# A four-layer trunk on one core: tile sizes and pools changed so that matmul operands begin at multiples of 128 bytes, with three steps moved in the feed-forward heads

## The chip, the cores and the metric

The kernel runs on one core of a Trainium2 chip. The metric is device time in microseconds for one execution. Before the change the median of three runs is 2381.13 us (2380.29 to 2392.86). A core has five engines that run side by side, each with an instruction stream of its own: TensorE (PE), VectorE (DVE), ScalarE (ACT), GpSimd (POOL) and SyncE (SP, which here only issues DMA transfers). Every time below comes from these runs, from the profile of one execution, or from its trace.

## What is computed

A batch of one with 512 positions of width 1024 goes through four layers. Each layer adds a mixer's output to `x` and then a gated feed-forward network (FFN):

```python
for layer in range(4):
    h = rmsnorm(x, norm_mix[layer])
    x = x + mixer(h)              # layers 0 and 3: S5; 1: GLA; 2: differential attention
    h = rmsnorm(x, norm_ffn[layer])
    g, u = split(h @ w_gate_up, 2)   # 1024 x 5632
    x = x + (silu(g) * u) @ w_down   # 2816 x 1024
return rmsnorm(x, norm_final)
```

All arrays are fp32. The S5 mixer is a diagonal state-space scan followed by a 1024 x 2048 product, GLA a gated linear attention with products of 1024 x 3088 and 1024 x 1024, the attention one with products of 1024 x 3072 and 1024 x 1024.

## The kernel before

**Products.** A large product is done in the type fp32r. Each operand is split into a high part and a remainder, and three matmuls (high by high, high by low, low by high) add up in PSUM: `mm3`, lines 349 to 353. A matmul has two SBUF operands. The stationary one is loaded into the array (128 columns, LDWEIGHTS), the moving one is streamed past it. In the profile a row `acc<-whl,act` names first what is written, then the moving operand (`whl`), then the stationary one (`act`).

- `gemm_b` (and `gemm_units`, its form as a generator): moving is a weight tile `whl` of 512 columns, stationary the activations (`act`, `hT`, `zT` or `oT`).
- `gemm_a`: moving is `hT`, the transposed normalised activations, 512 columns wide, and stationary the weights `whl`.
- `seven_product` (line 566): moving is a `side` of 256 columns, stationary the weights.

Weights come from HBM as fp32 (`staged`, tag `wst`), ACT casts the high part (line 334) and DVE subtracts it for the low part (line 338), both into `whl`.

**FFN of layers 1 to 3.** `ffn` computes the gate and up product with Strassen-like sums: seven half-size products instead of eight for each of 11 blocks of 256 hidden columns. `seven_block` gives the steps of a block: products `one` to `seven`, with sides "11", "1", "2", "12", "3", "4", "22" of the activations. Each product is 24 matmuls, so a block has 168. The sides "11" and "12" lie in a tile `sides` in the pool `hp`; the others, named `side1` and so on, lie in the FFN's own pool. The first two blocks ("heads" a and b) are interleaved in an order written out by hand, the string `plan` in `ffn`, and `hand_all` makes all engines keep that order until `hand()` gives it back to the scheduler. In `plan`, `split`, `high` and `low` are the ACT and DVE halves of making an operand, `add22` and `add21` are sums of weight tiles on DVE, `total1` to `total4` are sums of activation quarters on DVE, and `one:a` is product one of block a. After each 4, 4 and 3 blocks a `gemm_b` of the down projection runs. Some weight tiles are loaded twice, the second time by POOL's queue with an addition in flight (`load` with `plus`): names `room1` and `summed`.

**Turned x.** Layer 3 wants the rows of `x` in another order. `turn_x` (layer 2 only) writes `x` to DRAM and reads it back in the new order, 2 MB each way, and the same with the small `r`; all four DMAs go to POOL's queue, and the two that read wait there for those that write. It is called at block 2, tied behind the last adding DMA of that block by `issue_after`.

**Memory.** Pools are laid out one after another in SBUF in the order of `Trunk.__init__`: const, xp, hp, wp, normp (`np_`), small (`sp`), then the pool of the stage at work. A tile takes a multiple of 32 bytes in each partition. In front of const lie 8192 bytes of DMA scratch. The const pool adds up to 6080 bytes: four constants of the framework 128, `ident` 512, `mhalf` 32, `ones` 512, three columns 96, six S5 tables 1536, `pw` 2048, `dcol` 64, `mrow` 512, `mask16` 64, two rotation tables 512, two columns 64. That is 47 x 128 + 64, so xp begins 64 bytes past a multiple of 128, and so do hp, wp and every tile in them, whose sizes are multiples of 128. The table gives where each operand lies, as bytes past a multiple of 128:

| operand | pool | before | after the change |
|---|---|---|---|
| `whl` (weights), `hT`, `sides`, `x` | wp, hp, xp | 64 | 0 |
| `hh` (what is transposed) | normp | 64 | 0 |
| `act`, `side1` to `side22`, `oT` | stage pools | 0 | 0 |
| `zT` (S5) | right end of SBUF | 96 | 0 |
| `wa2`, `aT`, `kd`, `v`, `st`, `walr` (GLA) | gla | 32 | 0 |
| `X`, `Q`, `cs` of the first S5 layer | s5_0 | 32 | 0 |
| `X`, `Q` of the second, made beside layer 0's FFN | ffn0 | 64 | 0 |

The stage pools begin at a multiple of 128 before and after.

Of the kernel before, what the change touches and what calls it, by code (L numbers as in the profile page):

```python
# [21 lines left out]
P = 128  # L22
# [38 lines left out]
class Left:  # L61
# [84 lines left out]
class Sides(Left):  # L146
# [18 lines left out]
    def ahead(self, n):  # L165
# [3 lines left out]
        if len(self.heads) == 2:  # L169
            self.total("3")  # L170
# [49 lines left out]
class Chunks:  # L220
# [3 lines left out]
    def __init__(self, tr, grow):  # L224
# [3 lines left out]
        self.ms = tr.np_.tile([P, 2, NT], F32, tag="msq", name="msq")  # L228
# [13 lines left out]
    def finish(self):  # L242
# [6 lines left out]
        r = tr.np_.tile([P, NT], F32, tag="rcol", name="rcol")  # L249
# [13 lines left out]
class Trunk:  # L263
    def __init__(self, ctx, tc, ins, out):
# [177 lines left out]
    def normed(self, xt, g, out, pool, aside=False):  # L442
# [6 lines left out]
        ms = self.sp.tile([P, 1], F32, tag="ms", name="ms")  # L449
# [121 lines left out]
    def seven_block(self, fp, slots, left, wgu, b, turn):  # L571
# [20 lines left out]
        def load(name, q, half, plus=None, room=None):  # L592
# [8 lines left out]
            if plus:  # L601
                self.added = nc.gpsimd.dma_start(w[:], left.quarter(*plus, b), accum_op=ALU.add)
# [109 lines left out]
    def ffn(self, l, left, after=None, turn=False, aside=None):  # L712
# [5 lines left out]
        with self.tc.tile_pool(name=f"ffn{l}", bufs=1, reuse_waits="tile") as fp:  # L718
# [14 lines left out]
            for w, n, *room in (  # L733
# [6 lines left out]
                split21a one:a split21b square flush one:b total1 one_out:a finish high1 low1 total2 split1a high2 low2  # L740
                one_out:b two:a two:b split1b high3 two_out:a five:a add22a highSa two_out:b lowSa five_out:a five:b
                add22b highSb diag lowSb low3 split3a six:a spread five_out:b rows six:b six_out:a split3b seven:a
                six_out:b total4 split22a high4 low4 seven:b seven_out:a split22b three:a seven_out:b gate1:a gate1:b
                high22 low22 three:b add21a highFa add21b lowFa highFb lowFb four:a four:b three_out:a three_out:b
            """
            for step in plan.split():
# [11 lines left out]
                elif name == "flush":  # L758
                    self.flush()
                else:  # L760
# [7 lines left out]
            for nb in (4, 4, 3):  # L768
                acts = []
                for n in range(b0, b0 + nb):  # L770
# [29 lines left out]
    def turn_x(self, r):  # L800
# [8 lines left out]
        r = self.np_.tile([P, NT], F32, tag="rcol", name="rturned")  # L809
# [147 lines left out]
    def s5_rows_of_phases(self, p, cp, fhi, flo, f):  # L957
# [31 lines left out]
        self.mmagic = cp.tile([P, 1], F32, name="mmagic")  # L989
# [212 lines left out]
    def s5_spilled(self, pool, L):  # L1202
# [5 lines left out]
        rs = pool.tile([P, 1, 112], F32, name="rssp")  # L1208
# [172 lines left out]
    def s5_first(self, ctx):  # L1381
# [3 lines left out]
        zT = zpool.tile([P, 2, KT, SEQ], F32R, name="zT")  # L1385
# [752 lines left out]
```

## Time and profile before

The profiled execution took 2382.31 us, of which the span in the trace, from the first to the last instruction, is 2380.6 us.

| engine | busy us | share of the span |
|---|---|---|
| DVE | 1487.1 | 62% |
| ACT | 1073.0 | 45% |
| POOL | 266.8 | 11% |

The TensorE clock granted is 0.98 of full speed over the span. The core reads 275.92 MB from HBM and writes 23.99 MB. The line for TensorE and the rows for the largest groups stand in the prediction. A row of groups gives the line of the source, the engine, the operation, the names, the shape (partitions x elements), the number of instructions, then the busy time in us and the mean ns of one, and behind the second bar the idle time before them and what ended it. Matmuls overlap in the pipeline, so the mean duration of one (some 390 ns) isn't what it costs; that is the distance from one start to the next. A row of the timeline gives the start in us, the length in us, the engine, line, operation, names, shape and the count of merged instructions, and in brackets the idle time before it with its releaser.

### The profile page before, as it was taken

The page shows a single profiled execution, that of the slowest core. Times are in us where ns is not written, and L with a number is a line of the kernel's source. Part 1 is how long each engine was busy: PE and PEld are TensorE (multiplying, and loading weights), DVE is VectorE, ACT ScalarE, POOL GpSimd, SP SyncE. Part 2 cuts the span into 40 slices and gives each one's busy share as a digit, 9 for nine tenths or more (in the row PEclk, how much of TensorE's full clock was granted, in tenths as well). Part 3 has the DMA queues.
Part 4 walks back from the last instruction along what each step waited for, and adds up shares of the span by engine and source line. Part 5 has one row for each costly group of instructions (what it writes and reads, how often), then busy time and mean ns, then how long its engine had stood idle before and what let it go on. Part 6 is the DMA issues. An engine that isn't in the chain of part 4 may idle for free. (4 is left out here: it accounts for less than half of the span.)

```text
span 2380.6 us, 35208 instructions
## 1 busy us (share of the span) xinstructions
PE 2269.0 (95%) x14055; PEld 1962.8 (82%) x14055; DVE 1487.1 (62%) x2311; ACT 1073.0 (45%) x1749; POOL 266.8 (11%) x335
## 2 busy tenths in 40 slices
PE   4799999999999999999999998989999899999997
PEld 3578888788877789898987887888989788999996
DVE  7774565555443459585753666875847874967674
ACT  4463445444352346252544665653635233634442
POOL 3330100111000011010001221110000000101000
PEclk9699999999999999999999999999999899999999
DMA  4123344544332258564345465694732645666521
GB/s 110 34 52 138 95 138 143 166 129 166 118 103 85 71 143 208 137 177 124 111 142 117 107 133 145 170 243 115 195 98 89 214 158 150 170 179 154 162 76 67
DMA packets 275502, 317.42 MB, mean 133 GB/s; under 512 B 45653, under 2 KB 214377, under 8 KB 274058
## 3 DMA queue, kind: packets, MB, share of 16 engines
q1 hardware_dynamic: 227210, 238.14, 31.9%
q0 software_dynamic: 48128, 77.02, 15.7%
q8 instruction: 111, 1.82, 0.3%
q14 instruction: 53, 0.43, 0.1%
HBM read 275.92 MB, written 23.99 MB: 126 GB/s over the span
## 5 line engine op out<-in xcount | busy, mean ns | idle before, releaser
L338 DVE TENSOR_TENSOR whl<-wst,whl 128x1024 fp32r<-128x1024 f32 x294 | 359.0, 1223 | 363.1 <-ACT whl L334 362.3
L334 ACT CAST whl<-wst 128x1024 fp32r<-128x1024 f32 x294 | 308.4, 1050 | 530.5 <-PE acc L353 354.8
L566 PE MATMUL a<-side,whl 128*128 128x256 f32 x2376 | 291.2, 279 | 14.2 <-ACT r L638 6.0
L566 PEld LDWEIGHTS a<-side,whl 128*128 128x128 f32 x2376 | 281.4, 190 | 16.2 <-ACT whl L334 6.9
L351 PE MATMUL acc<-whl,act 128*128 128x512 f32 x704 | 276.5, 393 | 0.7 <-DVE g L611 0.7
L353 PE MATMUL acc<-whl,act 128*128 128x512 f32 x704 | 276.9, 393 | 0.0
L352 PE MATMUL acc<-whl,act 128*128 128x512 f32 x704 | 275.6, 391 | 0.0
L566 PE MATMUL c<-side,whl 128*128 128x256 f32 x1584 | 192.4, 278 | 3.6 <-DVE whl L338 3.6
L566 PEld LDWEIGHTS c<-side,whl 128*128 128x128 f32 x1584 | 186.9, 189 | 4.0 <-DVE whl L338 4.0
L351 PEld LDWEIGHTS acc<-whl,act 128*128 128x128 f32 x704 | 132.2, 188 | 30.9 <-DVE g L611 1.9
L352 PEld LDWEIGHTS acc<-whl,act 128*128 128x128 f32 x704 | 132.2, 188 | 28.8
L353 PEld LDWEIGHTS acc<-whl,act 128*128 128x128 f32 x704 | 132.3, 188 | 27.9
L351 PE MATMUL any<-hT,whl 128*128 128x512 f32 x384 | 151.7, 395 | 0.0
L352 PE MATMUL any<-hT,whl 128*128 128x512 f32 x384 | 149.6, 390 | 0.0
L353 PE MATMUL any<-hT,whl 128*128 128x512 f32 x384 | 149.6, 389 | 0.0
L351 PE MATMUL acc<-whl,hT 128*128 128x512 f32 x352 | 143.8, 408 | 1.1 <-ACT whl L334 0.6
L352 PE MATMUL acc<-whl,hT 128*128 128x512 f32 x352 | 138.6, 394 | 1.0 <-DVE whl L338 1.0
L353 PE MATMUL acc<-whl,hT 128*128 128x512 f32 x352 | 139.0, 395 | 0.0
L338 DVE TENSOR_TENSOR whl<-halves,whl 128x1024 fp32r<-128x1024 f32 x72 | 87.7, 1222 | 32.5 <-ACT whl L334 32.5
L352 PE MATMUL acc<-whl,zT 128*128 128x512 f32 x256 | 103.9, 406 | 4.1 <-DVE whl L338 4.1
L334 ACT CAST whl<-halves 128x1024 fp32r<-128x1024 f32 x72 | 75.3, 1052 | 69.2 <-PE acc L353 26.7
L351 PE MATMUL acc<-whl,zT 128*128 128x512 f32 x256 | 102.8, 406 | 2.7 <-ACT zT L468 2.7
(438 smaller groups left out, 4185.1 us busy)
## 6 DMA issues: line engine op xcount, KB each, us to landing
wst<-in_ffn_w_gate_up_dram SPq DMA_DIRECT2D x110, 512.0 KB, 4.0
wst<-in_ffn_w_down_dram SPq DMA_DIRECT2D x88, 512.0 KB, 3.7
halves<-in_ffn_w_gate_up_dram SPq DMA_DIRECT2D x42, 512.0 KB, 5.9
slot<-in_ffn_w_gate_up_dram SPq DMA_DIRECT2D x39, 512.0 KB, 6.6
wst<-in_ffn_w_gate_up_dram POOLq DMA_DIRECT2D x33, 512.0 KB, 6.4
wst<-in_s_w_glu_dram SPq DMA_DIRECT2D x32, 512.0 KB, 3.6
spill<-opsp POOLq DMA_DIRECT2D x8, 2048.0 KB, 8.7
wst<-in_gla_w_in_dram SPq DMA_DIRECT2D x24, 512.0 KB, 3.6
```

The source lines that it names most:

```text
L334: self.nc.scalar.copy(hl[:, 0], w[:])
L338: self.nc.vector.tensor_tensor(hl[:, 1], w[:], hl[:, 0].bitcast(F32), op=ALU.subtract)
L351: mm(out, lh, rh, start=first, stop=False)
L352: mm(out, lh, rl, start=False, stop=False)
L353: mm(out, ll, rh, start=False, stop=last)
L566: mm(o, hl[:, x, k, c], side[:, y, k], start=first and not (j or k or n), stop=k == 3 and n == 2, skip_group_check=True,)
```

## The change

Constants: `ones` is put ahead of `mhalf`, and `mhalf` grows from 8 to 24 columns (32 to 96 bytes), so the const pool is 6144 bytes, 48 x 128. The small tiles `msq` and `rcol` go from normp to the pool small, whose tile `ms` gets 6 buffers instead of 8: small goes from 1856 to 1920 bytes, normp loses 128. `mmagic`, `ind` and `rssp` are made wider (to 128, 128 and 512 bytes) and used as before. Behind `zT` at the right end of SBUF lies a new unused tile `edge` of 96 bytes.

Order in the FFN heads: `high22` and `low22` (side 22) come ahead of `three:a`, with `add21a` and its `high` and `low` behind them; before, they came after both `gate1` steps. `total3` is no longer called inside `ahead`: layers 1 and 3 call it right after `ahead(2)`, and layer 2 calls it in `plan`, ahead of `total1`. At the end of the attention layer the two evacuations `evac(0)` and `evac(1)` come two matmul groups sooner, and each `ahead(1)` follows the evacuation of its row block.

x's copy: `turn_x` is called in `plan`, behind `five:b`, instead of at block 2.

```diff
-        self.ms = tr.np_.tile([P, 2, NT], F32, tag="msq", name="msq")
-        self.r = tr.np_.tile([P, NT], F32, tag="rcol", name="rcol")
+        self.ms = tr.sp.tile([P, 2, NT], F32, tag="msq", name="msq", bufs=2)
+        self.r = tr.sp.tile([P, NT], F32, tag="rcol", name="rcol", bufs=2)
...
         self.heads += [self.tr.halves(y, 4, 256) for y in w]
-        if len(self.heads) == 2:
-            self.total("3")
...
-        self.mhalf = self.cp.tile([P, 8], F32, name="mhalf")
+        self.ones = self.cp.tile([P, P], F32, name="ones")
+        self.mhalf = self.cp.tile([P, 24], F32, name="mhalf")
         nc.vector.memset(self.mhalf[:], -0.5)
-        self.ones = self.cp.tile([P, P], F32, name="ones")
...
-        ms = self.sp.tile([P, 1], F32, tag="ms", name="ms")
+        ms = self.sp.tile([P, 1], F32, tag="ms", name="ms", bufs=6)
...
-                self.added = nc.gpsimd.dma_start(w[:], left.quarter(*plus, b), accum_op=ALU.add)
+                nc.gpsimd.dma_start(w[:], left.quarter(*plus, b), accum_op=ALU.add)
...
-                split21a one:a split21b square flush one:b total1 one_out:a finish high1 low1 total2 split1a high2 low2
+                split21a one:a split21b square flush one:b total3 total1 one_out:a finish high1 low1 total2 split1a high2 low2
                 one_out:b two:a two:b split1b high3 two_out:a five:a add22a highSa two_out:b lowSa five_out:a five:b
-                add22b highSb diag lowSb low3 split3a six:a spread five_out:b rows six:b six_out:a split3b seven:a
-                six_out:b total4 split22a high4 low4 seven:b seven_out:a split22b three:a seven_out:b gate1:a gate1:b
-                high22 low22 three:b add21a highFa add21b lowFa highFb lowFb four:a four:b three_out:a three_out:b
+                turn add22b highSb diag lowSb low3 split3a six:a spread five_out:b rows six:b six_out:a split3b seven:a
+                six_out:b total4 split22a high4 low4 seven:b seven_out:a split22b high22 low22 three:a add21a highFa
+                seven_out:b lowFa add21b gate1:a highFb three:b lowFb gate1:b four:a four:b three_out:a three_out:b
             """
+            if l != 2:
+                plan = plan.replace("total3", "")
...
+                elif name == "turn":
+                    r = self.turn_x(left.r) if turn else r
...
-                    if turn and n == 2:
-
-                        with self.tc.issue_after(self.added.ins):
-                            r = self.turn_x(left.r)
...
-        self.mmagic = cp.tile([P, 1], F32, name="mmagic")
+        self.mmagic = cp.tile([P, 32], F32, name="mmagic")[:, :1]
...
-        rs = pool.tile([P, 1, 112], F32, name="rssp")
+        rs = pool.tile([P, 1, 128], F32, name="rssp")[:, :, :112]
...
         zT = zpool.tile([P, 2, KT, SEQ], F32R, name="zT")
+        zpool.tile([P, 24], F32, name="edge")
...
-                ahead = (lambda: nxt.ahead(2)) if L and d else None
+                ahead = (lambda: (nxt.ahead(2), nxt.total("3"))) if L and d else None
...
-            ind = p.tile([P, 2], F32, name="ind")
+            ind = p.tile([P, 32], F32, name="ind")[:, :2]
...
-                2: {1: (one,), 3: (one, lambda: evac(0, banks[0])), 5: (one, lambda: evac(1, banks[1])), 7: (one,)},
-                3: {1: (one,), 3: (one, lambda: nxt[0].ahead(1)), 5: (one,)},
+                2: {1: (one, lambda: evac(0, banks[0])), 3: (lambda: evac(1, banks[1]), one), 5: (one,), 7: (one,)},
+                3: {1: (one,), 3: (one,), 5: (one,)},
...
                 evac(t, banks[t])
-                if t == 2:
-                    nxt[0].ahead(1)
+                nxt[0].ahead(1)
```

More of the change, by code (lines that the diff above doesn't have):

```diff
@@ L248, in finish @@
         v.tensor_scalar_add(ms[:], ms[:], 1e-6)
-        r = tr.np_.tile([P, NT], F32, tag="rcol", name="rcol")
+        r = tr.sp.tile([P, NT], F32, tag="rcol", name="rcol", bufs=2)
         nc.gpsimd.tensor_tensor(r[:], ms[:], tr.mhalf[:, :NT], op=ALU.pow)
@@ L808, in turn_x @@
         nc.gpsimd.dma_start(d[:].rearrange("(t p) -> p t", p=P), r[:])
-        r = self.np_.tile([P, NT], F32, tag="rcol", name="rturned")
+        r = self.sp.tile([P, NT], F32, tag="rcol", name="rturned", bufs=2)
         nc.gpsimd.dma_start(r[:], d[:].rearrange("(p t) -> p t", t=NT))
@@ L1465, in s5_second @@
         zT = zpool.tile([P, 2, KT, SEQ], F32R, name="zT")
+        zpool.tile([P, 24], F32, name="edge")
         with self.tc.tile_pool(name="s5_1", bufs=1) as p:
```

4 lines of the change are left out of this document (2 added, 2 removed).

## The prediction

> **What bounds the kernel now.** I read the page first: which engine is busy, and which groups make it so.
>
> ```profile
> span 2380.6 us, 35208 instructions
> PE 2269.0 (95%) x14055; PEld 1962.8 (82%) x14055; DVE 1487.1 (62%) x2311; ACT 1073.0 (45%) x1749; POOL 266.8 (11%) x335
> L566 PE MATMUL a<-side,whl 128*128 128x256 f32 x2376 | 291.2, 279 | 14.2 <-ACT r L638 6.0
> L566 PE MATMUL c<-side,whl 128*128 128x256 f32 x1584 | 192.4, 278 | 3.6 <-DVE whl L338 3.6
> L351 PE MATMUL acc<-whl,act 128*128 128x512 f32 x704 | 276.5, 393 | 0.7 <-DVE g L611 0.7
> L351 PE MATMUL any<-hT,whl 128*128 128x512 f32 x384 | 151.7, 395 | 0.0
> L351 PE MATMUL acc<-whl,hT 128*128 128x512 f32 x352 | 143.8, 408 | 1.1 <-ACT whl L334 0.6
> L351 PE MATMUL acc<-whl,zT 128*128 128x512 f32 x256 | 102.8, 406 | 2.7 <-ACT zT L468 2.7
> ```
>
> TensorE is the bound, and its own matmuls follow each other without a wait. Lines 351 to 353 go together, so the 512-wide groups count 2112 (`act`), 1152 (`any`), 1056 (`hT`) and 768 (`zT`). The list with shapes kept apart gives the rest: 1584 matmuls with `sides`, 384 with `oT`.
>
> ```profile
> L566 PE MATMUL a<-sides,whl 128*128 128x256 f32 x792 | 100.3, 283 | 0.0
> L566 PE MATMUL d<-sides,whl 128*128 128x256 f32 x792 | 100.0, 283 | 0.9 <-ACT whl L334 0.9
> L351 PE MATMUL acc<-whl,oT 128*128 128x512 f32 x128 | 53.4, 417 | 2.4 <-ACT oT L468 2.4
> ```
>
> What one costs is the distance between starts, read from the timeline.
>
> ```profile
> 229.04 0.40 PE L351 MATMUL acc<-whl,zT 128*128 128x512 f32 x1
> 235.34 0.40 PE L351 MATMUL acc<-whl,zT 128*128 128x512 f32 x1
> ...
> 284.97 0.39 PE L351 MATMUL any<-hT,whl 128*128 128x512 f32 x1
> 291.09 0.39 PE L351 MATMUL any<-hT,whl 128*128 128x512 f32 x1
> ...
> 882.86 5.92 PE L566 MATMUL d<-sides,whl 128*128 128x256 f32 x48
> 888.62 5.62 PE L566 MATMUL c<-side,whl 128*128 128x256 f32 x48
> 894.08 2.89 PE L566 MATMUL a<-side,whl 128*128 128x256 f32 x24
> ...
> 984.46 0.39 PE L351 MATMUL acc<-whl,act 128*128 128x512 f32 x1
> 991.33 0.39 PE L351 MATMUL acc<-whl,act 128*128 128x512 f32 x1
> ```
>
> Between the pairs lie 27, 27, 48, 48 and 30 matmuls: `zT` 233.3 ns, `any` 226.7, `d<-sides` 120.0, `c<-side` 113.75, `act` 229.0. The middle pair decides: same shape, same weights pool, back to back; `sides` begins 64 bytes past a multiple of 128, `side` at one, and it costs 6.25 ns less. From 120.0 and 226.7, both 64 off, 256 more columns cost 106.7 ns. So 256 columns cost 106.7, 32 columns (128 bytes) 13.3, and the fixed part is 13.3 where the moving operand is off, as if one more stretch of 128 bytes were read, and 7.0 where it is aligned.
>
> **Part 1, the layout.** Afterwards both operands lie at 0. No row shows that pair for fp32r. The fixed part F lies between 0 (columns don't stream faster than in these rows) and 7.0 (moving at 0, weights still at 64). The lowest 512-wide distance is the one with both operands at the same phase (`any`, 64 and 64), while `act` (64 and 0) and `zT` (64 and 96) cost more; equal phases will hold everywhere afterwards, so I go below 7.0, to the middle: F = 3.3. Then a 512-wide matmul costs 216.7 and a 256-wide one 110.0. The gains: `zT` 16.6, `any` 10.0, `hT` taken as `any` 10.0, `act` 12.3, `oT` taken as `act` 12.3, `sides` 10.0, `side` 3.75.
>
> [...]
>
> Not all of it passes on. These rows show where another engine is near:
>
> ```profile
> 879.91:960.98 81.07, 77.03 (x660) 76.00 (x658) 72.05 (x83) 48.16 (x62) 10.06 (x8) 1.00 0.77 197
> 1508.11:1600.44 92.33, 80.79 (x659) 79.83 (x658) 76.42 (x91) 53.24 (x70) 12.78 (x12) 0.94 0.89 234
> 2028.87:2110.30 81.43, 78.25 (x660) 77.43 (x659) 73.06 (x84) 50.11 (x64) 10.06 (x8) 0.98 0.78 198
> ...
> 1400.00:1475.00 75.00, 67.40 (x398) 54.67 (x397) 55.70 (x151) 55.17 (x154) 15.70 (x22) 1.00 0.48 115
> 1858.00:1950.00 92.00, 82.92 (x585) 76.21 (x582) 82.81 (x119) 22.84 (x35) 1.05 (x1) 0.93 0.64 228
> ```
>
> Columns: stretch, length, then busy PE, PEld, DVE, ACT, POOL, granted clock, DMA share, GB/s. The first three are the stretches of blocks 0 to 3 in the three FFNs; DVE is busy 72 to 76 us there, so I count half. In the attention PE has gaps (67.4 of 75): 60%. In the S5 pipe of layer 3 DVE works 82.8 of 92 us; the 192 `zT` matmuls of the two pipes count nothing. Elsewhere all passes.
>
> - `zT`: 576 x 16.6 ns = 9.6 us
> - `any`: 1152 x 10.0 = 11.5
> - `hT`: 480 in GLA, 4.8; 576 in the attention, 5.8 x 0.6 = 3.5
> - `act`: 2112 x 12.3 = 26.0
> - `oT`: 192 in GLA, 2.4; 192 in the attention, 1.4
> - FFN blocks: 1584 x 10.0 + 3960 x 3.75 = 30.7; 4 of 11 blocks count half: 25.1
>
> Sum 84.3 us, on about 9500 matmuls that pass on; each ns of F is worth 9.5 us. F = 0 would add 31, F = 7.0 take 35. The wider tiles and `edge` add no instruction; one memset at the start, of `mhalf`, grows by 16 columns, before TensorE has its first work. The tiles moved between the small pools keep two buffers, and `ms` with six has at most four users in a row (the four row blocks of a norm), so no wait comes of it. What is left of TensorE's work (transposes, scores, the S5 matmuls in plain fp32) I count at nothing: those groups are small, none is among the eight rows above, and a gain there would fall mostly into the attention and the S5 pipes, whose rows follow.
>
> **Part 2, the heads.**
>
> ```profile
> 909.88 1.22 DVE L217 TENSOR_TENSOR side<-halves,side 128x1024 fp32r<-128x1024 f32 x1 [1.64 <-ACT side L212]
> ...
> 913.43 0.50 PE L566 MATMUL a<-side,whl 128*128 128x256 f32 x2 [1.95 <-ACT whl L334]
> 914.69 5.49 PE L566 MATMUL a<-side,whl 128*128 128x256 f32 x46 [0.76 <-DVE whl L338]
> 924.12 2.77 PE L566 MATMUL c<-side,whl 128*128 128x256 f32 x22 [0.84 <-DVE whl L338]
> ```
>
> `four:a` waits 2.7 us for side 22 and the sum of weights, because both are made after `gate1`. Made sooner, they are there when `three` ends. But the next wait, at 924.12, is for DVE's own queue, which had stood idle only 1.64 us; the remaining work on it is the same. I count 1.3 per head (between 0 and 2.7), 3.9 for three. At the end of the attention `total3` and the second head's split stood ahead of the last evacuation, and the transposes behind it waited:
>
> ```profile
> 1507.72 0.63 PE L108 MATMUL tp<-ident,hh 128*128 128x128 f32 x4 [1.69 <-ACT sq L99]
> ```
>
> Without them it falls away: 1.5 (0 to 1.7); `total3` then stands on DVE ahead of `total1`, whose product comes 5 us later.
>
> **Part 3, x's copy.** The FFN of layer 2 has 92.3 us in that stretch, the other two 81.1 and 81.4. What is late:
>
> ```profile
> 1511.41 1.03 POOL L126 TENSOR_TENSOR rcol<-ms,mhalf 128x4 f32<-128x4 f32 x1 [3.74 <-DVE ms L125]
> 1518.73 1.33 POOL L602 DMA_DIRECT2D halves<-in_ffn_w_gate_up_dram  x1 [6.29 <-DMA halves<-in_ffn_w_gate_up_dram]
> ...
> 1533.68 1.30 POOL L804 DMA_DIRECT2D xturn<-vall  x1
> 1555.97 0.57 POOL L806 DMA_DIRECT2D x<-xturn  x1 [12.53 <-DMA xturn<-vall]
> 1571.35 1.29 POOL L602 DMA_DIRECT2D wst<-in_ffn_w_gate_up_dram  x1 [9.24 <-DMA slot<-in_ffn_w_gate_up_dram]
> ...
> 1543.82 1.05 ACT L334 CAST whl<-halves 128x1024 fp32r<-128x1024 f32 x1
> ...
> 1580.64 1.04 ACT L334 CAST whl<-wst 128x1024 fp32r<-128x1024 f32 x1 [7.09 <-DMA wst<-in_ffn_w_gate_up_dram]
> ...
> 1584.54 5.02 PE L566 MATMUL a<-side,whl 128*128 128x256 f32 x24 [6.04 <-ACT r L638]
> ...
> 1520.00:1530.00 10.00, 10.00 (x89) 9.93 (x88) 8.95 (x14) 6.99 (x10) 0.05 (x1) 1.00 0.39 64
> 1540.00:1550.00 10.00, 7.39 (x62) 7.18 (x63) 9.97 (x14) 7.36 (x11) 1.32 (x1) 1.00 1.09 349
> ```
>
> The copy out took 22 us amid full DMA engines (1.09), and the weight tile that PE needed came late; the wait also lowered the clock (24 matmuls took 5.02 us). Moved behind `five:b` the copy goes to POOL right behind `r` (1511.41), so all four DMAs start from about 1512.4, and run while the share is 0.39 (1520 to 1530). On POOL's queue block 2's first adding DMA now stands behind them, until the copy out has landed; In the profile it went out at 1518.73, before the copy, and ACT took its tile at 1543.82. A copy out of 12 us from 1512.4 on lets it go at about 1525, 6 us later; with some 9 us for a load of that kind (the 9.24 us wait in the row at 1571.35) it lands near 1534, 10 us early. If the copy out took 22 us again, it would land about when it is needed. SP's loads pass by POOL's queue and only share the DMA engines; those issued between 1512 and 1535 belong to blocks 2 and 3. Where `x` is next used, the first `gemm_b`, lies 65 us later. I take 10 of the 11.2 us, between -2 (that tile a little late, and nothing won) and 11.2.
>
> **Sum.** Against the profiled execution's own 2382.3 us (the median of the runs, 2381.1, is 1.2 below it): 84.3 + 3.9 + 1.5 + 10 = 99.7, so 2282 us.
>
> **Rivals.**
> - *Phases don't matter to each other*: F stays 7.0, as the aligned row has it. For it: it is the only aligned row. Against: `act` and `zT` differ though both have the same moving tile. 2282 + 35 = 2318 us.
> - *A stationary operand at 0 is itself dearer*, by the 2.3 ns that `act` stands above `any`: F = 9.3, 2282 + 57 = 2339 us.
> - *The change does not do what it says*: what separates `d` and `c` is their pool, not the phase, and only parts 2 and 3 bring anything: 2382 - 15 = 2367 us. Against it: the difference is close to half of 13.3 ns. [...]
> - *Slower*: both operands beginning on the same phase 0 collide, and each matmul pays one stretch (13.3 ns) above the aligned row: F = 20.3, (20.3 - 3.3) x 9.5 = 162 us above my forecast: 2444 us. It decides from F = 13.8, where the 99.7 us of the sum are used up. Against it: with both at phase 64 nothing above the 13.3 is seen.
>
> **Chances and range.** My forecast 0.58, with its own range 2248 (F = 0) to 2318; F at 7.0 0.25; stationary dearer 0.09; no effect of the phase 0.04; slower 0.04. The range 2248 to 2345 takes in the first three. What can be told from no change is about 0.5%, 12 us. All but the last case are faster by more, 2367 only just, so I give faster 0.94, same 0.02, slower 0.04.
>
> **What would show it.** In the trace after: `d<-sides` and `c<-side` at the same distance, 107 to 114 ns; all 512-wide groups within 2 ns of each other between 213 and 220; the three FFN stretches alike at 77 to 80 us; no wait over 1 us at `four:a`; the copy out landing in 12 us. Wrong would be 512-wide distances that stay at 227 and above, a 256-wide one above 114, or PE waiting for block 2's `five`.

## The result and the profile after

The changed kernel took 2399.97 us (median of 9 runs, 2395.45 to 2402.79), the kernel before 2383.86 (9 runs, 2380.29 to 2392.86): ratio 1.0063, 95% interval 1.0049 to 1.0076. It became 0.6% slower, clear of the spread of the runs. The profiled execution took 2402.79 us, its span is 2401.1: 20.5 above before.

The page of the changed kernel, engines first, then the groups (line numbers are 2 lower than before: `seven_product` is L564, `mm3` L349 to L351):

```profile
span 2401.1 us, 35215 instructions
PE 2292.8 (95%) x14055; PEld 1980.7 (82%) x14055; DVE 1488.0 (62%) x2311; ACT 1073.9 (45%) x1749; POOL 267.3 (11%) x335
L564 PE MATMUL a<-side,whl 128*128 128x256 f32 x2376 | 298.8, 282 | 2.5 <-DVE whl L336 2.5
L564 PE MATMUL c<-side,whl 128*128 128x256 f32 x1584 | 202.5, 285 | 10.6 <-DVE whl L336 10.6
```

The count of matmuls is the same and TensorE is busy 23.8 us longer: the time is in the matmuls themselves, and in the groups that were to gain. Idle time moved too: `a<-side` waits 2.5 us in all instead of 14.2, `c<-side` 10.6 instead of 3.6. The distances come from the timeline of the same kernel:

```profile
284.77 0.39 PE L349 MATMUL any<-hT,whl 128*128 128x512 f32 x1
289.08 0.39 PE L350 MATMUL any<-hT,whl 128*128 128x512 f32 x1
...
885.19 5.92 PE L564 MATMUL d<-sides,whl 128*128 128x256 f32 x48
890.95 5.86 PE L564 MATMUL c<-side,whl 128*128 128x256 f32 x48
896.65 3.01 PE L564 MATMUL a<-side,whl 128*128 128x256 f32 x24
...
983.75 0.39 PE L349 MATMUL acc<-whl,act 128*128 128x512 f32 x1
990.03 0.39 PE L349 MATMUL acc<-whl,act 128*128 128x512 f32 x1
```

Between the rows lie 19, 48, 48 (from 890.95 to 896.65) and 27 starts: `any` 226.8 ns (before 226.7), `d` 120.0 (120.0), `c` 118.75 (113.75), `act` 232.6 (229.0). What was to become shorter stayed, and `side` and `act` became longer.

By stage, windows of before, then of the changed kernel: the rows at 1005.75 and 1010.95 are blocks 4 to 7 of FFN1, where TensorE has no gap; those at 882.23, 1520.24 and 2041.17 the stretches of blocks 0 to 3, which the prediction has as 81.07, 92.33 and 81.43.

```profile
1005.75:1083.19 77.44, 77.44 (x673) 77.43 (x672) 61.49 (x69) 43.78 (x54) 7.73 (x6) 1.00 0.71 184
```

```profile
1010.95:1090.89 79.94, 79.94 (x674) 79.94 (x673) 61.66 (x69) 43.48 (x54) 7.73 (x6) 1.00 0.69 178
...
882.23:965.29 83.06, 79.14 (x659) 78.34 (x658) 72.00 (x83) 47.68 (x62) 10.05 (x8) 1.00 0.76 199
1520.24:1607.96 87.72, 81.61 (x659) 80.79 (x658) 77.73 (x93) 52.85 (x70) 12.78 (x12) 0.96 0.94 238
2041.17:2124.65 83.48, 80.01 (x659) 79.59 (x658) 72.29 (x84) 49.71 (x64) 10.03 (x8) 0.98 0.77 199
```

Only the stretch with x's copy is shorter (-4.6); the other two are 2 us longer. In it POOL and TensorE look like this (a line of three dots stands for rows left out):

```profile
1526.00 0.83 POOL L802 DMA_DIRECT2D xturn<-vall  x1
...
1538.12 1.08 POOL L804 DMA_DIRECT2D x<-xturn  x1
...
1555.83 0.56 POOL L808 DMA_DIRECT2D rturned<-rturn  x1 [15.84 <-DMA rturn<-rcol]
...
1563.39 0.40 PE L564 MATMUL c<-side,whl 128*128 128x256 f32 x2
1568.56 5.06 PE L564 MATMUL c<-side,whl 128*128 128x256 f32 x22 [4.77 <-DVE whl L336]
```

The copy out took 12 us (1526.00 to 1538.12) where it had taken 22, and the 6.04 us wait of before is gone. In its place stands a wait of 4.77 us ahead of block 2's `five`, and the 22 matmuls behind it took 5.06 us instead of 2.8.

### The profile page after: what moved, and what is told of

It reads as the page before. It is cut to its first block, busy times and chain, and to the rows that moved or that the text cites. A ratio compares the mean times of both kernels' runs of the same rounds, so it can differ in the third digit from the quotient of the medians.

```text
span 2401.1 us, 35215 instructions
## 1 busy us (share of the span) xinstructions
PE 2292.8 (95%) x14055; PEld 1980.7 (82%) x14055; DVE 1488.0 (62%) x2311; ACT 1073.9 (45%) x1749; POOL 267.3 (11%) x335
## 5 line engine op out<-in xcount | busy, mean ns | idle before, releaser
L564 PE MATMUL a<-side,whl 128*128 128x256 f32 x2376 | 298.8, 282 | 2.5 <-DVE whl L336 2.5
L564 PEld LDWEIGHTS a<-side,whl 128*128 128x128 f32 x2376 | 289.0, 189 | 3.5 <-DVE whl L336 3.3
L349 PE MATMUL acc<-whl,act 128*128 128x512 f32 x704 | 279.6, 397 | 1.1 <-DVE g L609 1.0
L351 PE MATMUL acc<-whl,act 128*128 128x512 f32 x704 | 278.0, 395 | 0.0
L564 PE MATMUL c<-side,whl 128*128 128x256 f32 x1584 | 202.5, 285 | 10.6 <-DVE whl L336 10.6
L564 PEld LDWEIGHTS c<-side,whl 128*128 128x128 f32 x1584 | 195.9, 192 | 11.4 <-DVE whl L336 11.4
L349 PEld LDWEIGHTS acc<-whl,act 128*128 128x128 f32 x704 | 132.6, 188 | 33.3 <-DVE g L609 2.3
L351 PEld LDWEIGHTS acc<-whl,act 128*128 128x128 f32 x704 | 132.6, 188 | 30.9
L349 PE MATMUL any<-hT,whl 128*128 128x512 f32 x384 | 151.7, 395 | 0.0
L351 PE MATMUL any<-hT,whl 128*128 128x512 f32 x384 | 149.6, 390 | 0.0
L349 PE MATMUL acc<-whl,hT 128*128 128x512 f32 x352 | 144.2, 410 | 1.3 <-DVE ro L1863 0.7
L351 PE MATMUL acc<-whl,hT 128*128 128x512 f32 x352 | 139.1, 395 | 0.0
L349 PE MATMUL acc<-whl,zT 128*128 128x512 f32 x256 | 102.6, 405 | 2.8 <-ACT zT L466 2.8
```

What stands on the lines that cost most here:

```text
L349: mm(out, lh, rh, start=first, stop=False)
L351: mm(out, ll, rh, start=False, stop=last)
L564: mm(o, hl[:, x, k, c], side[:, y, k], start=first and not (j or k or n), stop=k == 3 and n == 2, skip_group_check=True,)
```

## Experiments

Below, "distance" between addresses means the byte address of the moving operand less that of the stationary one, modulo 256, and a mean start distance is the mean over all starts of a class that follow each other without a wait.

**Each half by itself.** `e1_order_alone` is the changed kernel with every line of the layout as before; `e2_layout_alone` is the kernel before with those lines as changed.

```diff
  e1: the changed kernel, and
-        self.ones = self.cp.tile([P, P], F32, name="ones")
-        self.mhalf = self.cp.tile([P, 24], F32, name="mhalf")
+        self.mhalf = self.cp.tile([P, 8], F32, name="mhalf")
...
-        zpool.tile([P, 24], F32, name="edge")
  e2: the kernel before, and the same lines the other way
```

> The changed order (heads, attention's end, x's copy) on the layout of before. Theory P (the cost hangs on where the moving operand lies against the stationary one, not on either address alone) and theory S (a stationary operand at a multiple of 128 is dear) both put all of the loss on the layout: 256-wide matmuls with side at 113 to 114 ns as before, act at 229, and the time 5 to 9 us below before, some 2376 us, from the FFN heads. Theory O (the new order loses the time): 2390 us or more, with the layout's rows as before.

> The new layout on the order of before. Theories P and S: side 119 to 121 ns, act 232, zT 232 to 233, hT and any 227 to 228 as before; the time 21 to 26 us above before, some 2406 us. Theory O: within 5 us of before.

| run | median us (before beside it) | ratio, 95% interval |
|---|---|---|
| order alone | 2376.32 (2387.11) | 0.9961 (0.9945 to 0.9978) |
| layout alone | 2407.54 (2387.11) | 1.0086 (1.0060 to 1.0112) |

The layout costs 0.86% and the new order gains 0.39%; the two add up to 0.47%, and the change measured 0.63%, within the intervals. So the whole loss lies in the layout. In the layout run the mean start distances are those of the changed kernel: `side` 118.7 (order alone 113.9), `act` 232.6 (229.0), `oT` 232.6 (229.3), `any` 227.4 (227.3), `hT` 228.1 (228.1), `zT` 232.6 (233.2), `sides` 119.6 (119.4). Times their counts that is 3960 x 4.8 + 2112 x 3.6 + 384 x 3.3 + 1584 x 0.2 - 768 x 0.6 = 28 us, beside 26.1 between the spans (2406.7 and 2380.6).

The gain of the order isn't where its expectation put it, in the FFN heads. By windows of its trace the stretches of blocks 0 to 3 take 81.58, 86.38 and 82.05 us (before 81.07, 92.33 and 81.43): 6 us come from the stretch with x's copy, and the other two are 0.5 and 0.6 us longer. The profiled execution was the longest of the ten (2383.15 us), so its span shows none of the gain.

**What makes `side` dearer.** The layout moved the weights by 64 bytes and left `side` where it was. Either a stationary operand at 0 is dear in itself, or only the distance counts. `e3_stage64` keeps the weights at 0 and moves all stage pools up by 64 bytes:

```diff
         self.dp = ep("dram", 1, space=DRAM)
+        self.sp.tile([P, 16], F32, tag="spad", name="spad", bufs=1)
```

> The changed kernel with one unused tile of 64 bytes at the end of the pool small, so that the stage pools (side, act, oT) begin 64 past a multiple of 128 and the weights stay at 0. Theory P: the distance between side and weights modulo 128 is that of before again (64), so side falls back to 113 to 114 ns and act to 229; 2400 - 25 - 6 = about 2369 us. Theory S: the stationary weights still lie at 0, side stays at 119 to 121 ns; act, whose stationary operand is now at 64, falls to 227; about 2395 us.

Its timeline in FFN1, then its window of blocks 4 to 7 there:

```profile
887.47 5.62 PE L565 MATMUL c<-side,whl 128*128 128x256 f32 x48
892.93 2.88 PE L565 MATMUL a<-side,whl 128*128 128x256 f32 x24
```

```profile
1004.30:1081.97 77.67, 77.67 (x673) 77.67 (x672) 61.03 (x68) 43.70 (x54) 7.73 (x6) 1.00 0.72 183
```

`c` is back at 113.75, blocks 4 to 7 at 77.67, `act` at 229.0, and the kernel at 2378.88, 0.9964 (0.9951 to 0.9976). One unused tile of 64 bytes takes back the whole loss. It is the distance that counts.

**Then `sides` too.** If -64 is good for 256 columns, the large buffers with `sides` should lie 64 under the weights. `e4_hp64` is order alone with const 64 bytes shorter (three one-column tiles merged) and 64 bytes of room ahead of the weights, so that xp and hp lie 64 lower. It also keeps `edge`, so that `zT` lies at distance 64:

```diff
-        self.halfpi = cp.tile([P, 1], F32, name="halfpi")
+        cols = cp.tile([P, 3], F32, name="cols")
+        self.halfpi = cols[:, 0:1]
...
         self.wp = ep("wp", 3)
+        self.wp.tile([P, 16], F32, tag="wpad", name="wpad", bufs=1)
```

> The changed order on the layout of before, with the pools xp and hp (hT, sides) 64 bytes lower while the weights stay 64 past a multiple of 128, and zT at 0 instead of 96. Theory P: sides falls from 120 to 113 to 114 ns, any from 226.7 to about 220, hT (moving and stationary swapped) rises to about 229, zT falls from 233 to 229; 1584 x 6.3 + 1152 x 6.7 + 576 x 4.2 - 1056 x 2.3 ns = 17.7 us, so 14 to 18 us below the run with the order alone, some 2360 us. Theory S has the same for sides and any, because their weights stay at 64, and leaves hT at 227 or lets it rise to 229. A theory by which only the pool matters: sides stays at 120 and the time at 2376 us.

The timeline of `any`, then the window of blocks 4 to 7 of FFN1:

```profile
286.74 0.40 PE L350 MATMUL any<-hT,whl 128*128 128x512 f32 x1
293.04 0.39 PE L350 MATMUL any<-hT,whl 128*128 128x512 f32 x1
```

```profile
1015.51:1091.69 76.18, 76.18 (x673) 76.18 (x672) 59.82 (x67) 42.78 (x54) 7.73 (x6) 1.00 0.73 186
```

`sides` fell from 119.4 to 114.1 and blocks 4 to 7 to 76.18. But `any`, which reads the same buffers 512 wide, rose from 227.3 to 233.3 (6.30 us over 27 starts): 1152 x 6 = 7 us given back of the 1584 x 5.3 = 8.4. `hT` as the stationary operand rose from 228.1 to 229.4, 1 us, and `zT` fell from 233.2 to 229.4, 3 us. That leaves some 3 us, which the times can't tell from nothing: 2378.11, 0.9967 (0.9948 to 0.9985), beside 0.9961 of order alone. The 14 to 18 us expected were a miss: what is good for 256 columns is bad for 512.

**A table of distances.** `e5_phases` leaves the whole trunk out. It loads two tiles, and reads them in groups of 48 matmuls, 512 wide and 256 wide in turn, while the moving operand goes up in steps of 32 bytes:

```diff
+    for s in (0, 16, 8):
+        for m in range(0, 128, 8) if s == 0 else range(0, 128, 16):
+            wide(m, s)
+            narrow(m, s)
```

> The disputed cost by itself: the whole trunk is left out, and fp32r matmuls run back to back in the pattern of line 349 to 353 (two stationary tiles, two moving ones), in groups of 48 with 512 moving columns and 48 with 256, with the moving operand moved on by 32 bytes from pair of groups to pair, 0 to 480, against a stationary operand at 0, then by 64 bytes against one at 64 and at 32. Theory P: the same distance gives the same spacing whatever the stationary address; at equal phases 120 ns (256 columns) and 226.7 (512), at a distance of -64 (448) 113 to 114 and about 233, at +64 229 for 512. A theory in which the address of the stationary operand counts by itself: the rows with it at 64 differ from those with it at 0 at equal distance by 3 ns or more. Theory P leaves open where the least of each curve lies: if it is below 113 and 226, a better layout than either kernel's follows.

The timeline: three pairs of groups with the stationary operand at 0, at distances 0, 64 and 192, then the two 256-wide groups at distance -64 with the stationary operand at 64:

```profile
30.13 11.07 PE L43 MATMUL acc<-mov,sta 128*128 128x512 f32 x48
41.04 5.92 PE L53 MATMUL acc<-mov,sta 128*128 128x256 f32 x48
46.79 11.36 PE L43 MATMUL acc<-mov,sta 128*128 128x512 f32 x48
...
63.59 11.15 PE L43 MATMUL acc<-mov,sta 128*128 128x512 f32 x48
74.58 5.60 PE L53 MATMUL acc<-mov,sta 128*128 128x256 f32 x48
80.02 11.37 PE L43 MATMUL acc<-mov,sta 128*128 128x512 f32 x48
...
130.83 11.37 PE L43 MATMUL acc<-mov,sta 128*128 128x512 f32 x48
142.03 5.61 PE L53 MATMUL acc<-mov,sta 128*128 128x256 f32 x48
147.47 11.35 PE L43 MATMUL acc<-mov,sta 128*128 128x512 f32 x48
...
309.76 5.62 PE L53 MATMUL acc<-mov,sta 128*128 128x256 f32 x48
315.22 11.06 PE L43 MATMUL acc<-mov,sta 128*128 128x512 f32 x48
...
376.76 5.82 PE L53 MATMUL acc<-mov,sta 128*128 128x256 f32 x48
382.42 11.06 PE L43 MATMUL acc<-mov,sta 128*128 128x512 f32 x48
```

Each start less the one before, over 48 (10.91 / 48 = 227.3 and 5.75 / 48 = 119.8 for distance 0), gives with the stationary operand at 0:

| distance | 0 | 32 | 64 | 96 | 128 | 160 | 192 (-64) | 224 (-32) |
|---|---|---|---|---|---|---|---|---|
| 512 wide, ns | 227.3 | 233.3 | 229.0 | 233.5 | 233.3 | 234.2 | 233.3 | 233.1 |
| 256 wide, ns | 119.8 | 116.7 | 113.3 | 120.0 | 118.8 | 118.8 | 113.3 | 118.5 |

The second 256 bytes repeat the first (distance 256: 226.9 and 120.0). Every class of before and after fits its column: `any` at 0, `act` at 64 and then 128, `side` at -64 and then 128, `sides` at 0. With the stationary operand at 64, distance 0 is alike (226.9 and 119.8), but +64 costs 233.4 and 117.8, so distance isn't all of it. And -64 has two readings there: 113.75 ns the first time, with the moving operand at 0 (309.76 to 315.22), and 117.9 the second time, with it at 256 (376.76 to 382.42). In all kernels but the changed one, `e2`, `e3` and `e12` the weights lie 64 past a multiple of 128, so this is the case that counted for the next runs; they were planned with 113.5 alone. No column has 216 or 110.

**Every operand at its best column.** `e6_phases_chosen` is order alone with `sides` and `side` at -64 and everything read 512 wide at 0, by 64 bytes of room in the stage pools and a view of `hT` that begins 64 bytes into its tile; several small tiles have fewer buffers, which makes the room. `e7_r_first` is order alone with the two small transfers of `r` ahead of x's copy, `e8_old_heads` order alone with the heads in the old order, `e9_both` the first and second together.

```diff
  e6
-        self.hT = [self.tr.hp.tile([P, KT, SEQ], F32R, tag="hT", name=f"hT{z}") for z in range(2)]
+            self.tr.hp.tile([P, 4160], F32R, tag="hT", name=f"hT{z}")[:, 16:4112].rearrange("p (k n) -> p k n", k=KT)
...
+            if l < 3:
+                fp.tile([P, 16], F32, name="pad")
  e7
+        nc.gpsimd.dma_start(e[:].rearrange("(t p) -> p t", p=P), r[:])
+        nc.gpsimd.dma_start(r[:], e[:].rearrange("(p t) -> p t", t=NT))
         nc.gpsimd.dma_start(d[:].rearrange("(t p) c -> p t c", p=P), self.x[:])
  e8
-                six_out:b total4 split22a high4 low4 seven:b seven_out:a split22b high22 low22 three:a add21a highFa
-                seven_out:b lowFa add21b gate1:a highFb three:b lowFb gate1:b four:a four:b three_out:a three_out:b
+                six_out:b total4 split22a high4 low4 seven:b seven_out:a split22b three:a seven_out:b gate1:a gate1:b
+                high22 low22 three:b add21a highFa add21b lowFa highFb lowFb four:a four:b three_out:a three_out:b
```

> The order of the changed kernel with the places of before, and each operand moved to the distance that the table of phases measured as cheapest: sides 64 bytes below the weights (modulo 256), everything that is read 512 columns wide at the weights' own distance. Theory A (the distance between moving and stationary address, modulo 256, sets the start distance, alike in the kernel and in the table): both sides products 113.5 to 114.5 ns (order alone: a 119.3 and d 119.4), act, zT, oT, hT and any all 226.7 to 228.1 ns (order alone: 229.0, 233.2, 229.3, 228.1, 227.3); gain 1584 x 5.5 + 2112 x 1.8 + 768 x 6 + 384 x 2 = 18 us under order alone at full passing on, time 2358 to 2365, about 0.989 of before. Theory B (the table holds only for one group read over and over; in the kernel other things, DMA writes or other engines' reads, set the distances): classes stay within 1 ns of order alone, time 2372 to 2380.

> Order alone, with the two small transfers of r issued ahead of x's copy and not behind it. Theory Q (behind the 2 MB read r's write lies still, the wait for it holds POOL for 15.8 us and with it block 2's summed transfer, and TensorE then waits 4.8 us ahead of block 2's five): the 15.84 us wait on POOL falls below 4 us, block 2's summed is issued near 1540 and not 1556, the wait ahead of its five is gone, FFN2's stretch from one:c to the downs 46.2 -> 41.5 to 43, time 3 to 5 us under order alone (2371 to 2374, 0.994 to 0.9955 of before). Rival (the wait ahead of five comes from the 2 MB read itself, which fills the engines that block 2's loads use, whoever is issued first): that stretch stays at 45 to 47 and the time within 1 us of order alone.

> Order alone with the heads of the FFN written in the old order from split22a on; first sum, attention's end and x's copy stay as changed. Theory R (the new order of the heads only moves the wait from four:a to block 2's five): the 2.7 us ahead of four:a come back, the 2.9 us ahead of block 2's five fall to 0.8, FFN1 one:c 43.1 -> 41 and one:b 38.5 -> 40, FFN3 alike; time within 1.5 us of order alone. Rival (the new order does save its 1.3 us per head, and the wait ahead of five has another cause): 3 to 5 us over order alone.

> The chosen phases and r first together. By theories A and Q the two gains add: 18 + 4 us under order alone, 2354 to 2361, about 0.987 to 0.990 of before; if the sides made 5 ns faster turn waits on the halves' splits or on transfers into the bound, less than the sum: 2361 to 2368.

| run | median us (before 2386.09) | ratio, 95% interval |
|---|---|---|
| `e6_phases_chosen` | 2388.59 | 1.0003 (0.9988 to 1.0018) |
| `e7_r_first` | 2381.85 | 0.9980 (0.9963 to 0.9998) |
| `e8_old_heads` | 2378.02 | 0.9962 (0.9948 to 0.9975) |
| `e9_both` | 2390.57 | 1.0013 (0.9996 to 1.0030) |

`e6` missed by at least 24 us, though the 512-wide classes came as the table has them: `act` 227.1, `zT` 227.8, `any` 227.3. Two things went wrong. Its timeline in FFN1, in the heads and at block 4:

```profile
892.47 0.80 PE L570 MATMUL c<-side,whl 128*128 128x256 f32 x2 [4.02 <-ACT whl L337]
...
1014.18 2.99 PE L570 MATMUL a<-sides,whl 128*128 128x256 f32 x24
1017.00 2.99 PE L570 MATMUL c<-side,whl 128*128 128x256 f32 x24
```

The passes of 24 follow each other at 2.82 us, 117.5 ns a matmul (117.8 on the mean), at the distance -64 that gave 113.3 in the table. At -64 there are two spacings. Before, 152 of 162 such passes ran near 113.3 and 10 near 117.8; in `e4` 202 of 229 ran at the shorter one, in `e6` 76 of 227. In blocks 4 to 10, where TensorE never waits, each stretch of `e4` and `e6` between two down products keeps the spacing that it entered with. In the kernel before the longer one lasts at most until the next pass over `sides` (distance 0) and is short again behind it; with all sides at -64 no such pass comes. And FFN1's first weights came late: the `lent` tiles were asked for at 875.5 and not at 844.5 as in order alone, which made the stretch from product one of block b to block 2 48.0 us instead of 38.5. The 64 bytes of room moved the pool's tiles over others of GLA that come free later; that is argued, not tried, but `e11` below, which has no such room, doesn't have this wait (38.1). The fewer buffers of `e6` haven't been tried apart from it. `e9` has both of `e6`'s faults (blocks 0 to 3 of FFN1 take 92.5 us, in order alone 81.6; blocks 4 to 7 are at the longer spacing) and missed by at least 22 us.

`e7`: theory Q fell. POOL no longer waits 15.8 us for `r`, and TensorE waits as in order alone, 4.87 us. Its timeline, engines together:

```profile
1524.69 0.58 POOL L804 DMA_DIRECT2D rturned<-rturn  x1 [9.08 <-DMA rturn<-rcol]
...
1545.70 1.04 ACT L332 CAST whl<-halves 128x1024 fp32r<-128x1024 f32 x1
...
1555.65 1.21 DVE L336 TENSOR_TENSOR whl<-halves,whl 128x1024 fp32r<-128x1024 f32 x1
...
1556.91 3.35 PE L564 MATMUL c<-side,whl 128*128 128x256 f32 x14 [4.87 <-DVE whl L336]
```

The high half of the awaited tile was there at 1546.7; DVE made the low half 9 us later, behind the last operations of blocks 0 and 1. Nor was it `r` that held this tile's load: in order alone POOL issues its adding DMA at 1531.75, ahead of `r`'s write, and what stands behind `r` is `summed`, the load for product seven. The wait is 1.9 us longer than in FFN1 and FFN3 (2.99 each). In this layer DVE writes `act` in twice as many parts for the turned rows (128x256, 0.58 to 0.63 us each, where the other two have 128x512 at 0.68), which would explain the rest; that is argued only.

`e8`: with the old order the 2.99 us ahead of block 2's `five` are gone and 1.96 and 0.55 us at `four:a` are back. The time is that of order alone, but both intervals are wider than the 3 to 5 us that the rival named. That the new order gains nothing rests on the stretches as well: in order alone they take 81.58 and 82.05 us in FFN1 and FFN3, in the kernel before, with the old order, 81.07 and 81.43.

A second effect shows in `e8`'s matmuls behind the wait (timeline) and in the granted clock there (windows, third number from the end):

```profile
917.65 0.71 PE L564 MATMUL a<-side,whl 128*128 128x256 f32 x2 [1.96 <-ACT whl L332]
918.91 8.22 PE L564 MATMUL a<-side,whl 128*128 128x256 f32 x46 [0.55 <-DVE whl L336]
```

```profile
914.35:917.76 3.41, 1.45 (x13) 1.25 (x13) 3.38 (x4) 1.10 (x2) 0.00 (x0) 1.00 1.14 291
917.00:922.00 5.00, 3.81 (x16) 3.52 (x17) 4.97 (x6) 3.53 (x4) 1.29 (x1) 0.58 1.09 360
```

The same wait in the kernel before, as windows:

```profile
909.61:913.02 3.41, 1.86 (x17) 1.67 (x15) 3.14 (x3) 0.93 (x2) 0.00 (x0) 1.00 1.16 253
913.02:916.44 3.42, 2.25 (x17) 2.05 (x18) 3.39 (x5) 3.30 (x4) 1.30 (x1) 1.00 1.09 366
```

The same pause cost 2.7 us more in `e8` (8.22 against 5.49 for 46 matmuls): the clock fell to 0.58 over 5 us, and not at all in the kernel before. In the kernel before all changes of the clock, from 1.00 to 0.50 and back, lie at multiples of 3.41 us from each other, and the windows of 3.41 us follow that grid. In `e8` the clock means of 0.58 (917 to 922) and 0.74 (922 to 927) are those of a clock at 0.50 for 6.83 us from 917.76 on, the end of its window. There the pause falls into that one window, which leaves 1.45 us of work in it. In the kernel before the grid cuts the pause in two (1.86 and 2.25 us of work). All seven falls of that trace between 1200 and 2100 us follow a window with 1.84 us of work or less; the one at 721.88 us follows a window that TensorE's busy time fills, so the work in the window ahead doesn't account for every fall.

**Earlier splits.** `e10_early2` is order alone with block 2's loads and first two splits written at the end of `plan`, so that DVE makes them ahead of the heads' last element products. `e11_phases_early2` adds `sides` at -64, `hT` and `zT` at 0, fewer buffers for a few small tiles, and no room in any stage pool.

```diff
+            for w in ("direct", "room1", "room22", "room21", "summed"):
+                blocks[2][w]()
+            blocks[2]["split"]("11")
+            blocks[2]["split"]("1")
             self.hand()
```

> Order alone, and block 2's loads and the splits of its first two products written into the heads' order, ahead of the heads' last products of elements. Theory D (the waits ahead of block 2's five, 2.99 in FFN1 and FFN3 and 4.87 in FFN2, are VectorE's queue: the low half that PE waits for stands behind some seven to ten operations of blocks 0 and 1, while its data and its high half have been there for 8 to 10 us): all three waits fall below 1 us and nothing takes their place, because the delayed operations are first needed by the down products 40 us later; time 2.0 + 2.0 + 4 = 7 to 10 us under order alone, 0.9925 to 0.9935 of before. Rival (the wait is the load: block 2's summed weights land too late): the waits stay at 2 us or more, or move to block 2's six, and the time stays within 2 us of order alone.

> Order alone with the early splits, and distances chosen anew: the sides in the two large buffers 64 bytes under the weights (modulo 256) as the stage's sides are, hT and zT at the weights' own distance, act and oT left 64 away as before, no room added in any stage's pool. Theory A with memory (at distance -64 a stretch runs at 113.3 or at 117.8 and keeps what it entered with; coming from the downs at distance 64 it enters at 113.3): both sides products 113.3 to 114.5, zT 227 to 228, any and hT 227 to 228, act 229, FFN blocks 4 to 7 76.2 and 8 to 10 57.1, S5's stretch 68.6; 9 + 4.5 us under the early splits alone, 2352 to 2360, 0.986 to 0.9895 of before. Rival (distance alone doesn't set it, 113 or 118 come by chance of the stage): blocks 4 to 7 at 79 as in the run with all phases chosen, and no gain of the sides: 2366 to 2374.

`e10`: 2379.47 (before 2385.85), 0.9979 (0.9969 to 0.9988): no gain over order alone, so theory D's forecast fell. In FFN1 the 2.99 us became two waits, and in FFN2 3.6 of the 4.87 us stay (timeline, FFN1 first, then FFN2 with its engines together):

```profile
920.29 2.90 PE L564 MATMUL a<-sides,whl 128*128 128x256 f32 x22 [1.20 <-DVE whl L336]
...
927.38 0.50 PE L564 MATMUL a<-side,whl 128*128 128x256 f32 x2 [1.68 <-ACT whl L332]
...
1538.72 0.55 POOL L811 DMA_DIRECT2D rturned<-rturn  x1 [13.24 <-DMA rturn<-rcol]
...
1551.25 1.04 ACT L332 CAST whl<-halves 128x1024 fp32r<-128x1024 f32 x1 [3.36 <-DMA halves<-in_ffn_w_gate_up_dram]
...
1552.35 0.50 PE L564 MATMUL c<-side,whl 128*128 128x256 f32 x2 [3.61 <-ACT whl L332]
```

The two have different causes. In FFN1 both waits end with DVE's work: the first with a low half, the second with a high half whose sum DVE had just made. There the order only chose which product waits. In FFN2 the wait is for a load: ACT waited 3.36 us for the adding DMA of the awaited tile, which POOL issued only at 1539.26, behind its 13.24 us wait for `r`. In `e7` and order alone that DMA goes out before the second half of x's copy (1527.84 and 1531.75) and DVE's queue is what ends last. So in FFN2 two limits lie close together, and a run that takes away both (early splits and `r` first) is missing. Over the span TensorE stands idle for 111.5 us (2376.7 less 2265.2 busy), in order alone for 111.1.

`e11`: 2375.69, 0.9965 (0.9944 to 0.9986), at least 15 us above what was expected. Blocks 4 to 7 of FFN1 and FFN3, whose operands lie at the same distances, as windows:

```profile
1003.82:1082.96 79.14, 79.14 (x673) 79.14 (x672) 61.56 (x69) 43.38 (x54) 7.73 (x6) 1.00 0.71 179
...
2149.90:2226.08 76.18, 76.18 (x673) 76.17 (x672) 60.12 (x68) 43.20 (x54) 7.69 (x6) 1.00 0.72 186
```

In FFN2 they take 79.15 us, and blocks 8 to 10 behind them, with the sides where they were, are back at the shorter spacing (57.1 us, in FFN1 59.4). So of blocks 4 to 7 two stretches ran at 117.8 ns and one at 113.3, in one execution; all three come behind the same kind of down product. My theory that the stage ahead decides fell with it. What chooses the spacing stays open.

**The version to keep.** `e12_stage64_zt` is the changed kernel with the stage pools 64 bytes up, as in `e3`, and `zT` 128 bytes lower, at distance 0:

```diff
+        self.sp.tile([P, 16], F32, tag="spad", name="spad", bufs=1)
...
-        zpool.tile([P, 24], F32, name="edge")
+        zpool.tile([P, 56], F32, name="edge")
```

> The changed kernel with every stage's pool 64 bytes higher, as in the run before that did this, and zT 128 bytes lower, so that it lies at the weights' own distance (modulo 256). By the table of phases and the two runs with zT there: zT from 232.3 to 227 to 228 ns, 768 x 4.6 = 3.5 us, S5's two stretches 70.2 to 68.6 each, everything else as in the run with the stages 64 higher; 2373 to 2378, 0.9935 to 0.9965 of before, under the changed kernel by about 1 per cent. Rival (what entered one stretch at one distance is given back in another, as in the runs with all phases chosen): S5's stretches 68.6, but FFN blocks 4 to 7 of one layer or more at 79 and not 77.7, time 0.996 to 0.999.

2373.63 us (before 2385.76), 0.9948 (0.9934 to 0.9962): faster than both kernels, by 0.5% and about 1%. `zT` is at 227.8 ns; in the two S5 layers its matmuls take 74.6 and 74.2 us from the first start to the last (76.0 and 75.6 in `e3`), 2.8 us together, and blocks 4 to 7 stay at 77.7, 77.7 and 77.4. Against `e3` (0.9964) and order alone (0.9961) the intervals overlap: that it is the fastest of the three rests on the distances and these stretches, not on the times.

## Why the prediction was wrong

**Part 1, the layout: the fixed part F, and with it the sign.** The step that failed reads `d` at 120.0 and `c` at 113.75 as "13.3 where the moving operand is off" and "7.0 where it is aligned", and then takes F = 3.3 for equal phases. What separates the two is the distance to the weights, modulo 256 and not 128: 0 for `d`, -64 for `c`. The table of before already held what equal phases cost: `d` and `any` had them, 64 and 64, at 120.0 and 226.7, which is F = 13.3; moving both to 0 changed neither. Nor is there one F for both widths: less 106.7 ns for each 256 columns, the table leaves 13.1 and 13.9 ns at distance 0 (256 and 512 columns), but 6.6 and 19.9 at -64. The layout brought `hT` and `sides` from distance 0 to 0, and `side`, `act` and `oT` from distances that suit them to 128. Term by term, per matmul, forecast gain and measured: `any` 10.0 and 0; `hT` 10.0 and 0; `sides` 10.0 and -0.2; `act` 12.3 and -3.6; `oT` 12.3 and -3.3; `side` 3.75 and -4.8; `zT` 16.6 and 0.6. The sum of 84.3 us became a loss of 20 (0.86% of 2387; 26 in the spans).

The slower rival named a collision of equal phases from F = 13.8 on. Equal phases do cost 13.3 at 256 columns, but they did so before as well; the loss came from operands that were not at equal phase modulo 256. The rival "a stationary operand at 0 is dear" fell with `e3`: the weights stay at 0 there, and `side` is back at 113.75. "The change does not do what it says" put the time at 2367 from parts 2 and 3 alone; that part of it, order alone, gave 0.39%, 9 us, of the 15.

In the table nothing but the addresses of the operands separates 113.3 from 119.8 ns for the same group of 48 matmuls; what in the chip makes the difference, no run shows. The 110.0 and 216.7 ns of the forecast lie under every column: the shortest were 113.3 and 226.9.

**Part 2, the heads.** At `four:a` no wait over 1 us is left, as forecast (the `a<-side` products wait 2.5 us in all three FFNs together). But the 1.3 us per head were not gained: the wait stands ahead of block 2's `five`, 2.9 us for 0.84. The prediction had named that wait and DVE's unchanged work, and still counted half; by the stretches of order alone, 0.5 and 0.6 us longer in FFN1 and FFN3 than before, it is nothing. The attention's end brought 1.87 for 1.5 (product one of block a in FFN2, with what stands in it, 5.09 to 3.22 us).

**Part 3, x's copy.** The mechanism was right: copy out in 12 us, the late tile in time, the 6.04 us gone. The size was off: from 92.3 to 86.4 in order alone, 6 of the 10 us taken. What is missing is DVE's queue ahead of block 2's `five`, 4.87 us, with the slow clock behind it (0.50 from 1562 to 1567 us in order alone); the finer split of the turned layer makes it probably longer there than in the other two layers, with which the prediction compared. POOL's 15.8 us wait for `r` looked like the cause and isn't, as the kernel stands (`e7`); with the splits made earlier it becomes one (`e10`).

**What would show it.** The text named as wrong: 512-wide distances of 227 and above, a 256-wide one above 114, TensorE waiting for block 2's `five`. All three came. The stretches came at 83 to 88, not 77 to 80.

## What to carry to other kernels

Measure what a matmul costs from start to start, and list it by the distance between its two operands modulo 256 bytes before any address is moved; that both begin at multiples of 128 doesn't settle it. A shift of one pool by 64 bytes, one unused tile, was worth about 1% here (`e3`), and a distance that is best for 256 columns (-64, 113.3 ns) is a bad one for 512 (233.3, where 0 has 227.3). Where one engine's work bounds a stretch, a new order can move the wait to the next product, as here from 2.7 us at `four:a` to 2.99 ahead of block 2's `five`: count that engine's work before counting a gain.

## What had not been expected of the hardware

- With fp32r and a weight load for each matmul, the distance between starts went with moving less stationary address modulo 256 (`e5`): 226.9 to 234.2 ns at 512 columns, 113.3 to 120.0 at 256. The stationary address itself counts too: at +64 it is 229.0 and 113.3 with that at 0, 233.4 and 117.8 with that at 64.
- At -64 and 256 columns there were two spacings, 113.3 and 117.8, that lasted over many passes (76.18 us for blocks 4 to 7 of FFN1 in `e4`, 79.14 in `e6`); the same sides ran at one and then at the other (FFN2 of `e11`), and the table has both with the stationary operand at 64.
- The small write of `r` (512 elements of 4 bytes, turned) kept POOL waiting for 9.08 us ahead of x's copy (`e7`), and for 15.84 us behind the 2 MB read (the changed kernel).
- Of two like pauses on TensorE one was followed by a clock of 0.50 for 6.83 us, the other by no fall: the first (2.5 us, `e8`) left 1.45 us of work in one window of 3.41 us, the second (2.7 us, the kernel before) left 1.86 and 2.25 in two. The changes of the clock lie on a grid of 3.41 us (the kernel before).
